# Second pass of the attention scores as 64-row matmuls on the two halves of the array, with every second tile of keys stored with its parts exchanged

## The chip, the cores and the metric

The kernel runs on one core of one Trainium2 chip. The metric is device time in microseconds, from the first to the last instruction of one execution; the number for a kernel is the median of its runs. Lower is better. PE is TensorE's matmul stream, PEld its weight loads, DVE VectorE, ACT ScalarE, POOL GpSimd, SP the engine that issues nearly all DMAs.

## What is computed

One decoder layer over 2048 tokens of width 1024: a conditioned RMS norm, one wide input projection, an mLSTM group of 4 heads, a differential-attention group of 8 heads, an output projection with a gate, and a final RMS norm. The change touches only the attention group, so this is the part to have in mind:

```python
def diff_attention(q, k, v, lam, rel_bias):
    q = q * (A_QKD ** -0.5)                       # A_QKD = 64, A_VHD = 128
    for blk in range(S // Q_BLOCK):               # 16 blocks of 128 queries
        ke = (blk + 1) * Q_BLOCK
        logits = einsum('bqhmd,bkhmd->bmhqk', q[blk], k[:, :ke])   # m: two maps
        logits = where(causal, logits + bias, -inf)
        p = softmax(logits, axis=-1)
        w = p[:, 0] - lam * p[:, 1]
        outs.append(einsum('bhqk,bkhe->bqhe', w, v[:, :ke]))
```

## The kernel before, in words

**Order of work.** Nothing is issued directly. `Program.note` writes every instruction down with what it reads and writes; `Program.order` then makes a list schedule from the planner's own costs (`Program.cost`, line 141): whenever a modelled engine is free, it takes the first noted instruction whose operands are there. The result is a fixed order for each engine, and the chip runs each engine's list in that order. So a cost in `cost` moves instructions, and changes no duration on the chip. All instructions therefore carry one line of the file, L243, and groups are told apart by the names of tiles.

**Stages.** `phase_a(0)` projects queries, keys, values and gates of the first 1024 tokens, `attention(0)` treats query blocks 0 to 7 of all heads, `phase_a(1)` and `attention(1)` do the same for the second 1024 tokens and blocks 8 to 15, and then come the mLSTM stages and the output projection. The scheduler mixes neighbouring stages: while attention waits for other engines, PE takes projection matmuls (PSUM tiles `ps_pj`), which are noted later and so have lower priority.

**Precision.** Every projected value is kept as two parts, hi and lo, both float32r, whose sum is the value. `keep_qk` (line 712) writes the parts of 64 channels of one map to DRAM, `dQ` and `dK`, in the order hi, lo.

**Scores** (`attention`, lines 854 to 875). For a head, K is loaded so that partitions 0 to 63 hold its hi part and 64 to 127 its lo part (`Kt`, in the arena `ar`). Q is loaded twice, so that `Qt[:, m, 0]` holds Q hi in both halves, and `Qt[:, m, 1]` Q lo in both. One tile of up to 512 keys takes two matmuls into one bank of PSUM: the first gives Q hi times (K hi + K lo), the second adds Q lo times (K hi + K lo). The banks `ps_S` are four, taken in turn. After a tile's second matmul DVE takes its minimum (`tensor_reduce` or `tensor_tensor_reduce`, into `mn`); after the last tile of a map ACT takes the exponential of every tile, which frees the banks. A query block has 1 to 4 tiles.

**What follows.** The weights `w` are turned on PE (`ps_tr`), split into parts, and multiplied by V (`ps_pv`).

Of the kernel before, what the change touches and what calls it, by code (L numbers as in the profile page):

```python
# [14 lines left out]
DRAM = bass.MemoryType.DRAM  # L15

P = 128
# [50 lines left out]


class Lane:  # L70
    """One engine's instruction stream: calls are noted down, not issued."""

    def __init__(self, prog, name):
        self.prog, self.name = prog, name
# [5 lines left out]


class Program:
    """Notes the kernel's instructions with what they read and write, then issues them in the
    order of a list schedule: whenever an engine is free it takes the first noted instruction
    whose operands are there."""

    LANES = ("tensor", "vector", "scalar", "gpsimd", "sync")
    COLD = 32000.0
# [52 lines left out]
    def cost(self, lane, method, out, ins, kwargs):  # L141
        n = self.width(out)
        if lane == "sync":
            return 530.0
        if lane == "tensor":
            if method == "transpose":
                return 109.0
            if ins[0].dtype == F32R:
                return max(108.0, 3 + n / 2.4)
            return 2 * max(108.0, 3 + n / 1.2)  # L150
        if lane == "scalar":
            aps = sum(isinstance(kwargs.get(k), bass.AP) for k in ("scale", "bias", "accum_out"))
            return 51.0 + n / 1.2 + 93.0 * aps
        n = max(n, max((self.width(a) for a in ins), default=0))
        if lane == "gpsimd":
            if kwargs.get("op") == ALU.pow:
                return 300.0 + 165.0 * n
            return 150.0 + n * (2.1 if method == "tensor_tensor" else 0.9)
        scalars = [a for a in ins if self.width(a) == 1]
        if method in ("tensor_scalar", "tensor_copy") and "PSUM" not in str(ins[0].space):  # L160
            return 68.0 + n * 0.53
        if method == "reciprocal":
            return 60.0 + n * 8
        return 68.0 + n * 1.042 + (62.0 if scalars else 0.0)
# [81 lines left out]
class K:  # L246
# [172 lines left out]
        nc.vector.tensor_scalar(tmp, src, scale, EPS, op0=ALU.mult, op1=ALU.add)  # L419
        nc.gpsimd.tensor_tensor(dst, tmp, self.half[:, :n], op=ALU.pow)  # L420

# [1 line left out]
    def ht(self, slot, lo):  # L423
        return self.r(self.hs[slot] + lo * 4096, [KT, 512])

# [1 line left out]
        return self.r(W0 + lo * 3136, [KT, 392])  # L427

    def turned(self, n, vecs):
        """vectors over channels, turned so that channels lie on partitions"""  # L430
        nc = self.nc
        parts = vecs[-1][0] + vecs[-1][1].shape[0] // P
        rows = self.f(MST + 512 + n * P, [P], parts=parts)
        if n == 0:
            nc.gpsimd.memset(rows, 0.0)
        for at, src in vecs:
            nc.sync.dma_start(out=rows[at:at + src.shape[0] // P, :], in_=src.rearrange("(k p) -> k p", p=P))
        pt = self.psum("pj" if n == 0 else "tr")
        nc.tensor.transpose(pt[:, 0:parts], rows, self.ident[0:parts, 0:parts])
        nc.vector.tensor_copy(self.cols[:, 72 * n:72 * n + parts], pt[:, 0:parts])  # L440
# [12 lines left out]
        self.gsc = cst.tile([P, KT], F32, name="gsc")  # L453

    def adaln(self, g, on_pe):
        """shift and scale of 256 channels: some of the products on TensorE, the others on VectorE"""
        nc = self.nc
        acc = self.f(SML + 512 * (g % 2), [2, 256])
        m = len(on_pe) + 1
        pm = self.psum("md")[:, 0:4 * m].rearrange("p (q j i) -> p q j i", q=2, j=2)  # L460

        def columns(i, src, vec):
            for q in (1, 0):
                for j in range(2):
                    nc.tensor.matmul(pm[:, q, j, i:i + 1], src[:, q, j * P:(j + 1) * P], vec, start=True, stop=True)

        for k in range(KT):
            slab = self.f((0, 2048, MST)[(2 * g + k // 4) % 3] + k % 4 * 512, [2, 256])
            rows = self.i["w_ada"][0, k * P:(k + 1) * P, 0:2048]
            nc.sync.dma_start(out=slab, in_=rows.rearrange("p (q c) -> p q c", q=2)[:, :, g * 256:(g + 1) * 256])  # L470
            sc = self.sc[:, k:k + 1]
            if k in on_pe:
                columns(on_pe.index(k), slab, sc)
            elif k == 0:
                nc.vector.tensor_scalar(acc, slab, sc, None, op0=ALU.mult)
            else:
                nc.vector.scalar_tensor_tensor(acc, slab, sc, acc, op0=ALU.mult, op1=ALU.add)
        columns(m - 1, acc, self.ones[:, 0:1])
        ks = slice(2 * g, 2 * g + 2)
        for q, dst in ((1, self.gsc), (0, self.shift)):  # L480
            if m > 1:
                nc.vector.tensor_reduce(dst[:, ks], pm[:, q], axis=AX.X, op=ALU.add)
            nc.vector.tensor_tensor(dst[:, ks], dst[:, ks] if m > 1 else pm[:, q, :, 0],
                                    self.cols[:, 32 + 8 * q + 2 * g:34 + 8 * q + 2 * g], op=ALU.add)
        nc.vector.scalar_tensor_tensor(self.gsc[:, ks], self.gsc[:, ks], 1.0,
                                       self.cols[:, 64 + 2 * g:66 + 2 * g], op0=ALU.add, op1=ALU.mult)

    def load_x(self, tg):
        """x of four token tiles, scaled by its reciprocal root mean square"""
        nc = self.nc  # L490
        x = self.i["x"][0]
        junk = self.f(TMP, [1024])
        ss, tmp, rr = (self.hst[:, q, 4 * tg:4 * tg + 4] for q in range(3))
        for j in range(4):
            t = tg * 4 + j
            xt = self.f((0 if tg == 1 else 4096) + 1024 * j, [1024])
            nc.sync.dma_start(out=xt, in_=x[t * P:(t + 1) * P, :])
            nc.scalar.activation(junk, xt, AF.Square, accum_out=ss[:, j:j + 1])
            self.rsqrt(rr[:, j:j + 1], ss[:, j:j + 1], 1.0 / D, 1, tmp[:, j:j + 1])
            nc.vector.tensor_scalar(xt, xt, rr[:, j:j + 1], None, op0=ALU.mult)  # L500
# [29 lines left out]
                                           in_=self.dH[tg][lo][:, q:q + 2, :])  # L530

    def out_gate(self):
        """the output gate on all partitions, kept in DRAM"""
        nc = self.nc
        ga, gb = self.f(4096, [1024]), self.f(5120, [1024])
        for k in range(KT):
# [12 lines left out]
        nc.sync.dma_start(out=self.dB, in_=gb)  # L549

    def gate_weights(self):
        """the gates' columns, beside the last slot of the weight ring"""
        nc = self.nc
        gw = self.f(TMP + 1024, [KT, 8])
        nc.sync.dma_start(out=gw, in_=self.i["w_in"][0, :, C_MI:C_MI + 8].rearrange("(k p) c -> p k c", p=P))
# [84 lines left out]
        nc.scalar.activation(self.g_ws, self.g_ws, AF.Exp)  # L640
        nc.scalar.activation(self.g_dc, self.g_dc, AF.Exp)

# [1 line left out]
    def fill_w(self, c0, hi, lo, eng=None):  # L644
        nc = self.nc
        raw = self.f(RAW + (self.nw % 2) * 1024, [KT, P])
# [12 lines left out]
        return self.wring(0)[:, :, cs], self.wring(1)[:, :, cs]  # L659

    def load_w2(self, c0, *slots):
        """256 columns in one load: two slots of the ring, or one wide one"""
        nc = self.nc
        raw = self.f(RAW, [KT, 256])
        nc.sync.dma_start(out=raw, in_=self.i["w_in"][0, :, c0:c0 + 256].rearrange("(k p) c -> p k c", p=P))
# [6 lines left out]
        return ws  # L672

    def proj_c(self, w, slot, name):
        """channel-major block: [128 channels, 512 tokens]"""
        pj = self.psum("pj", name)
        self.proj_k(pj, w, slot, range(KT))
        return pj
# [8 lines left out]
            nc.tensor.matmul(pj, lo[:, k, :], h0[:, k, :], start=False, stop=(k == KT - 1))  # L687

    def proj_t(self, w, slot, j2, name):
        """token-major block: two tiles of [128 tokens, 256 columns]"""  # L690
        pj = self.psum("pj", name)
        for j in range(2):
            self.proj_r(pj[:, j * 256:(j + 1) * 256], w, slot, 2 * j2 + j)
# [15 lines left out]
            o = MST + self.nst * 1024  # L709
        return self.f(o, [512], F32R), self.f(o + 512, [512], F32R), self.f(o, [2, 512])  # L710

    def keep_qk(self, pj, dst, tg, scale, at=None):
        nc = self.nc
        hi, lo, both = self.stage_a(at)
        self.split(hi, lo, pj, scale)
        ts = slice(tg * 512, (tg + 1) * 512)
        for m in range(2):
            nc.sync.dma_start(out=dst[2 * m:2 * m + 2, :, ts].rearrange("s p c -> p s c"),
                              in_=both[64 * m:64 * m + 64])

    def phase_a(self, half, mid, first=()):
        nc = self.nc
        tgs = (2 * half, 2 * half + 1)
        stage = self.stage_a

        def heads_qk(c0, slots, dsts, scale, ws):
            done = ws is not None
            for w, dst in zip(ws or self.load_w2(c0, *slots), dsts):
                for tg in tgs[1:] if done else tgs:
                    self.keep_qk(self.proj_c(w, tg % 2, ""), dst, tg, scale)  # L730

        def head_z(h, w):
            for tg in tgs:
# [8 lines left out]
        for pr in range(AH // 2):  # L742
            h0 = 2 * pr
            pre = (first[0:2], first[2:4]) if first and pr == 0 else (None, None)
            heads_qk(C_AQ + P * h0, (c, a), self.dQ[h0:h0 + 2], -0.125, pre[0])
            heads_qk(C_AK + P * h0, (1, c), self.dK[h0:h0 + 2], 1.0, pre[1])
            w, = self.load_w2(C_AV + 256 * pr, min(a, 1))
            if pr == 1:
                w = tuple(self.wring(j)[:, :, P:] for j in range(2))
# [24 lines left out]
                break  # L774
        self.wa, self.wc = a, c

# [1 line left out]
    def bias_tiles(self):  # L778
        nc, cst = self.nc, self.cst
        rb = cst.tile([33, AH], F32, name="rb")  # L780
# [9 lines left out]
        for h in range(AH):  # L790
# [3 lines left out]
            nc.vector.tensor_copy(sb, pb[:, 0:384])  # L794
            dst = self.dT[h].rearrange("(p c) -> p c", c=513)[:, 0:384]
            nc.sync.dma_start(out=dst, in_=sb)

    def attention(self, half):
        nc, cst = self.nc, self.cst
# [25 lines left out]
        for h in range(AH):  # L825
# [7 lines left out]
            for pi in range(4 * half, 4 * half + 4):  # L833
# [7 lines left out]
                for bq in range(2):  # L841
# [12 lines left out]
                    for m in range(2):  # L854
# [1 line left out]
                        mn, nm = mnt[sid2], nmt[sid2]  # L856
                        pts = []
                        npart = 0
                        for (a, bnd) in tiles:
                            pt = self.psum("S", f"ps_S{h}_{i}_{m}_{a}")  # L860
                            pts.append(pt)
                            for s in range(2):
                                nc.tensor.matmul(pt[:, 0:bnd - a], Qt[:, m, s, bq * P:(bq + 1) * P],
                                                 Kt[:, m, a:bnd], start=(s == 0), stop=(s == 1))
                            f1 = min(bnd, Fc)
                            if f1 > a:
                                nc.vector.tensor_reduce(mn[:, npart:npart + 1], pt[:, 0:f1 - a], axis=AX.X, op=ALU.min)
# [63 lines left out]
                nc.vector.scalar_tensor_tensor(c_, turned, self.anw, zt, op0=ALU.mult, op1=ALU.mult)  # L931
                nc.sync.dma_start(out=self.dA[pi // 2][:, h, (pi % 2) * 256:(pi % 2 + 1) * 256], in_=c_)

# [1 line left out]
    def stage_m(self):  # L935
        self.nst = (self.nst + 1) % 3
        o = (MST, MST + 1040, TMP)[self.nst]
# [72 lines left out]
        for n in range(8):  # L1010
            self.zo(half, n, *((c, a), (1, c), (a, 1))[n % 3])

# [1 line left out]
    def mlstm_buffers(self):  # L1014
        nc, cst = self.nc, self.cst
        self.ml_f = (self.f(0, [8, P]), self.f(1024, [4, 256]), [self.f(2048 + 512 * j, [4, P]) for j in range(2)],
# [222 lines left out]
```

## Time and profile before

| | |
|---|---|
| median of 3 runs | 2996.12 us |
| lowest and highest | 2994.66 and 2997.53 us |
| the profiled execution: span from first to last instruction | 2997.5 us |
| PE busy | 2849.1 us (95%) in 16032 matmuls |
| PEld busy | 2454.4 us (82%) |
| DVE, ACT, POOL busy | 1649.4, 1351.0, 914.4 us |

The profiled execution is as long as the slowest of the three runs and 1.4 us above their median. "Busy" for PE counts a matmul from its start to a modelled end, and matmuls overlap in it: a record of 0.40 us follows the one before it after 0.23 us. So what one matmul costs in a row of its kind is read from the distance of starts, not from the duration. A weight load (PEld) normally lies under the matmul before it. "issue" as the cause of idle time means that the engine waited for nothing that the profile shows.

### The profile page before, as it was taken

What the parts mean: (1) busy time and instruction counts of PE and PEld (TensorE: products, weight loads), DVE (VectorE), ACT (ScalarE), POOL (GpSimd) and SP (SyncE); (2) the same over time, 40 slices, a digit from 0 to 9 for tenths busy, and PEclk for the clock granted to TensorE, in tenths of its full rate; (3) what the DMA queues carried; (4) which work ended last, traced back from release to release, by engine and by line L of the source; (5) the groups of instructions that cost most, each with busy time, mean ns of one, the idle gap of its engine ahead of it and who ended that gap; (6) DMA issues with size and microseconds to landing.
All of it is one profiled execution on the core that took longest, in us unless ns stands there. A gap on an engine that the chain in (4) does not pass through costs nothing.

```text
span 2997.5 us, 43354 instructions
## 1 busy us (share of the span) xinstructions
PE 2849.1 (95%) x16032; PEld 2454.4 (82%) x16032; DVE 1649.4 (55%) x3378; ACT 1351.0 (45%) x3355; POOL 914.4 (31%) x594
## 2 busy tenths in 40 slices
PE   7999999999999999999999999999989889999999
PEld 5878888888888888798887888788788877878887
DVE  6123327776711557766866767866777575232222
ACT  4111325565611455565655656664554454221211
POOL 3112232322312232231221232233544454243332
PEclk9999999999999999999999999999999999999999
DMA  7356667666654632334253335524433444333332
GB/s 257 110 164 231 222 214 218 176 163 176 182 171 123 210 96 87 100 103 115 75 130 84 109 102 190 148 78 123 133 117 98 143 126 150 103 124 115 126 115 97
DMA packets 407539, 419.96 MB, mean 140 GB/s; under 512 B 19540, under 2 KB 348446, under 8 KB 405278
## 3 DMA queue, kind: packets, MB, share of 16 engines
q1 hardware_dynamic: 407326, 417.19, 46.7%
q8 instruction: 126, 2.06, 0.3%
q14 instruction: 87, 0.71, 0.1%
HBM read 280.77 MB, written 136.35 MB: 139 GB/s over the span
## 4 chain that ended last, share of the span: by engine, by line
PE 75%; DVE 10%; DMA 7%; ACT 3%; issue 3%; POOL 2%; SPq 1%; POOLq 0%; DVEq 0%; ACTq 0%
PE ps_pj L243 51%; PE ps_S L243 12%; DVE af L243 7%; PE ps_pv L243 7%; PE ps_tr L243 5%; DMA ar<-dK 3%; ACT af L243 2%; POOL ar L243 1%; ACT ar L243 1%; DVE ar L243 1%; DMA ar<-dQ 1%; SPq L243 1%; DMA af<-in_w_in_dram 1%; DMA ar<-dV 1%; DVE mn L243 1%
## 5 line engine op out<-in xcount | busy, mean ns | idle before, releaser
L243 PE MATMUL ps_pj<-ar 128*128 128x512 f32 (+2 forms) x9936 | 2162.6, 363 | 6.5 <-POOL ar L243 3.1
L243 PEld LDWEIGHTS ps_pj<-ar 128*128 128x128 f32 x9936 | 1648.1, 190 | 268.7 <-issue 5.3
L243 POOL TENSOR_TENSOR ar<-af,ar 128x1024 fp32r<-128x1024 f32 (+3 forms) x308 | 627.9, 2048 | 1068.6 <-ACT ar L243 934.4
L243 PE MATMUL ps_S<-ar 128*128 128x512 f32 (+4 forms) x2096 | 527.6, 357 | 42.3 <-DMA ar<-dK 22.4
L243 ACT ACTIVATE af<-ps_S,nm 128x512 f32<-128x512 f32 (+2 forms) x608 | 386.8, 642 | 141.4 <-DVE nm L243 92.0
L243 ACT ACTIVATE ar<-af 128x1024 fp32r<-128x1024 f32 (+3 forms) x321 | 285.7, 907 | 342.1 <-PE ps_pj L243 201.7
L243 PEld LDWEIGHTS ps_S<-ar 128*128 128x128 f32 x2096 | 351.2, 197 | 91.4 <-issue 33.7
L243 DVE TENSOR_REDUCE mn<-ps_S 128x1 f32<-128x512 f32 (+3 forms) x512 | 297.6, 589 | 146.5 <-PE ps_S L243 143.6
L243 ACT ACTIVATE af<-ps_pj 128x512 f32<-128x512 f32 (+2 forms) x292 | 171.2, 586 | 431.6 <-PE ps_pj L243 385.4
L243 PE MATMUL ps_pv<-ar 128*128 128x256 f32 (+2 forms) x1920 | 319.7, 283 | 20.4 <-DVE af L243 9.2
L243 POOL TENSOR_SCALAR af<-af,rZ,nlam 128x128 f32<-128x128 f32 (+15 forms) x128 | 168.3, 1315 | 529.4 <-DVE rZ L243 445.8
L243 PEld LDWEIGHTS ps_pv<-ar 128*128 128x128 f32 x1920 | 280.5, 190 | 56.7 <-DVE ar L243 16.2
L243 ACT ACTIVATE ar<-ps_tr 128x512 fp32r<-128x512 f32 (+1 forms) x288 | 165.7, 575 | 236.3 <-PE ps_tr L243 226.0
L243 DVE TENSOR_TENSOR ar<-ps_tr,ar 128x512 fp32r<-128x512 f32 (+1 forms) x288 | 188.8, 656 | 113.4 <-ACT ar L243 112.6
L243 DVE SCALAR_TENSOR_TENSOR af<-af,rZ 128x128 f32<-128x128 f32 (+15 forms) x128 | 193.8, 1514 | 27.6 <-POOL af L243 27.3
L243 DVE SCALAR_TENSOR_TENSOR af<-af,cols 128x512 f32<-128x512 f32 x192 | 189.7, 989 | 30.8 <-ACT af L243 28.8
L243 PE MATMUL ps_tr<-ident,af 128*128 128x128 f32 x1115 | 184.8, 277 | 12.9 <-DVE af L243 12.4
L243 DVE TENSOR_TENSOR af<-ps_pj,af 128x512 fp32r<-128x512 f32 (+3 forms) x103 | 66.3, 643 | 186.1 <-ACT af L243 174.7
L243 ACT ACTIVATE af<-af 128x512 f32<-128x512 f32 (+3 forms) x114 | 78.1, 685 | 181.8 <-DVE af L243 176.7
L243 PEld LDWEIGHTS ps_tr<-ident,af 128*128 128x128 f32 x1115 | 134.4, 142 | 26.3 <-DVE af L243 16.5
L243 POOL TENSOR_TENSOR ss<-ss,half 128x2 f32<-128x2 f32 x64 | 48.9, 764 | 337.4 <-DVE ss L243 286.8
L243 DVE TENSOR_TENSOR ps_pj<-ps_pj,af 128x512 f32<-128x512 f32 (+1 forms) x33 | 22.6, 683 | 206.2 <-PE ps_pj L243 206.2
(135 smaller groups left out, 1748.0 us busy)
## 6 DMA issues: line engine op xcount, KB each, us to landing
af<-in_w_in_dram SPq DMA_DIRECT2D x50, 1024.0 KB, 5.1
ar<-dQ SPq DMA_DIRECT2D x128, 256.0 KB, 4.2
af<-in_w_in_dram SPq DMA_DIRECT2D x44, 512.0 KB, 5.0
af<-in_x_dram SPq DMA_DIRECT2D x32, 512.0 KB, 3.8
dQ<-af SPq DMA_DIRECT2D x64, 256.0 KB, 4.8
dK<-af SPq DMA_DIRECT2D x64, 256.0 KB, 3.9
dV<-af SPq DMA_DIRECT2D x64, 256.0 KB, 2.2
dH<-ar SPq DMA_DIRECT2D x32, 512.0 KB, 6.1
```

The costliest lines, as they stand in the source:

```text
L243: getattr(getattr(nc, lane), method)(*args, **kwargs)
```

## The change

The second matmul of a tile now leaves out Q lo times K lo: it reads only the 64 rows in which K hi lies. For that to be possible on either half of the array, K tiles of every second 512 keys are written to `dK` with their parts exchanged, so that K hi lies in partitions 64 to 127 there. A static method, `aside`, finds neighbouring tiles of which each lies in one block of 512 keys and which lie in opposite kinds of block. Their second matmuls are noted after all first matmuls of the map, as matmuls of 64 rows, one on rows 0 to 63 and one on rows 64 to 127 (the program gives them a tile of 64x128 at row 0 or 64). All other tiles keep the full second matmul, which is right for either order of the parts, since Q lies in both halves. DVE's minima are noted after all of a map's matmuls. The planner is told that a float32r matmul with 64 rows costs 60 + n/4.8 ns, which is 167 ns for 512 columns where the full one is put at 216.

```diff
@@ cost
             if ins[0].dtype == F32R:
+                if ins[0].shape[0] == 64:
+                    return 60 + n / 4.8
                 return max(108.0, 3 + n / 2.4)
@@ keep_qk
-    def keep_qk(self, pj, dst, tg, scale, at=None):
+    def keep_qk(self, pj, dst, tg, scale, at=None, turn=False):
         for m in range(2):
-            nc.sync.dma_start(out=dst[2 * m:2 * m + 2, :, ts].rearrange("s p c -> p s c"),
-                              in_=both[64 * m:64 * m + 64])
+            if turn:
+                for s in range(2):
+                    nc.sync.dma_start(out=dst[2 * m + 1 - s, :, ts], in_=both[64 * m:64 * m + 64, s, :])
+            else:
+                nc.sync.dma_start(out=dst[2 * m:2 * m + 2, :, ts].rearrange("s p c -> p s c"),
+                                  in_=both[64 * m:64 * m + 64])
@@ phase_a (keys only)
-                    self.keep_qk(self.proj_c(w, tg % 2, ""), dst, tg, scale)
+                    self.keep_qk(self.proj_c(w, tg % 2, ""), dst, tg, scale, turn=keys and tg % 2 == 1)
@@ new
+    @staticmethod
+    def aside(tiles):
+        of, ti = [], 0
+        while ti + 1 < len(tiles):
+            (a, b), (c, d) = tiles[ti:ti + 2]
+            if (a // 512 + 1 == c // 512) and (b - 1) // 512 == a // 512 and (d - 1) // 512 == c // 512:
+                of += [ti, ti + 1]
+                ti += 1
+            ti += 1
+        return of
@@ attention
-                        for (a, bnd) in tiles:
+                        qs = slice(bq * P, (bq + 1) * P)
+                        aside = self.aside(tiles)
+                        for ti, (a, bnd) in enumerate(tiles):
                             pt = self.psum("S", f"ps_S{h}_{i}_{m}_{a}")
                             pts.append(pt)
-                            for s in range(2):
-                                nc.tensor.matmul(pt[:, 0:bnd - a], Qt[:, m, s, bq * P:(bq + 1) * P],
-                                                 Kt[:, m, a:bnd], start=(s == 0), stop=(s == 1))
+                            nc.tensor.matmul(pt[:, 0:bnd - a], Qt[:, m, 0, qs], Kt[:, m, a:bnd],
+                                             start=True, stop=False)
+                            if ti not in aside:
+                                nc.tensor.matmul(pt[:, 0:bnd - a], Qt[:, m, 1, qs], Kt[:, m, a:bnd],
+                                                 start=False, stop=True)
+                        for ti in aside:
+                            a, bnd = tiles[ti]
+                            rows = slice(a // 512 % 2 * 64, a // 512 % 2 * 64 + 64)
+                            nc.tensor.matmul(pts[ti][:, 0:bnd - a], Qt[rows, m, 1, qs], Kt[rows, m, a:bnd],
+                                             start=False, stop=True)
+                        for pt, (a, bnd) in zip(pts, tiles):
                             f1 = min(bnd, Fc)
```

What this does to the order of instructions shows at three places. Both programs have 15856 matmuls. The order prints a matmul's output only, so a tile's first matmul and its 64-row second one read alike.

The first place is PE in `attention(1)`: the second map of query block 9 of one head, with tiles of 512, 512 and 256 keys in banks `ps_S2`, `ps_S3` and `ps_S0`. Before:

```order
L243 MATMUL ps_S2_135<-ar_131 128x512 x2
L243 MATMUL ps_pj0_139<-ar_131 128x256
L243 MATMUL ps_pv_138<-ar_131 128x256 x5
L243 MATMUL ps_tr_137<-ident_141,af_132 128x128 x4
L243 MATMUL ps_pj0_139<-ar_131 128x256 x10
L243 MATMUL ps_S3_136<-ar_131 128x512 x2
L243 MATMUL ps_pv_138<-ar_131 128x256
L243 MATMUL ps_pj0_139<-ar_131 128x256
L243 MATMUL ps_pj1_140<-ar_131 128x256 x4
L243 MATMUL ps_S0_133<-ar_131 128x256 x2
```

The same three tiles after the change:

```order
L245 MATMUL ps_S2_135<-ar_131 128x512 x2
L245 MATMUL ps_pj0_139<-ar_131 128x256 x7
L245 MATMUL ps_S3_136<-ar_131 128x512 x2
L245 MATMUL ps_pj0_139<-ar_131 128x256
L245 MATMUL ps_pv_138<-ar_131 128x256
L245 MATMUL ps_pj0_139<-ar_131 128x256 x5
L245 MATMUL ps_S0_133<-ar_131 128x256
L245 MATMUL ps_pv_138<-ar_131 128x256 x5
L245 MATMUL ps_tr_137<-ident_141,af_132 128x128 x4
L245 MATMUL ps_S0_133<-ar_131 128x256
```

The tiles in `ps_S2` and `ps_S3` are a pair of `aside`, but a bank comes free at a time, so the 64-row matmul of each stands right behind its own first matmul, with seven projection matmuls between the two. The second place, also PE in `attention(1)`, is a pair whose two banks (`ps_S3` and `ps_S0`) are free together. Before:

```order
L243 MATMUL ps_S3_136<-ar_131 128x512
L243 MATMUL ps_pv_138<-ar_131 128x256 x5
L243 MATMUL ps_tr_137<-ident_141,af_132 128x128 x4
L243 MATMUL ps_S3_136<-ar_131 128x512
L243 MATMUL ps_S0_133<-ar_131 128x512 x2
```

After:

```order
L245 MATMUL ps_tr_137<-ident_141,af_132 128x128 x4
L245 MATMUL ps_S3_136<-ar_131 128x512
L245 MATMUL ps_S0_133<-ar_131 128x512
L245 MATMUL ps_S3_136<-ar_131 128x512
L245 MATMUL ps_S0_133<-ar_131 128x512
L245 MATMUL ps_pj1_140<-ar_131 128x512 x2
```

Here the two 64-row matmuls stand next to each other. The third place is SP in `phase_a(0)`, the stores of one head's keys (`dK_77`) for two token blocks. Before:

```order
L243 DMA dK_77<-af 64x2x512 x2
L243 DMA af<-in_w_ada_dram 128x1024 x2
L243 DMA dK_77<-af 64x2x512 x2
L243 DMA af<-in_w_in_dram 128x8x256
```

After:

```order
L245 DMA dK_77<-af 64x2x512 x2
L245 DMA af<-in_w_ada_dram 128x1024 x2
L245 DMA dK_77<-af 64x512 x4
L245 DMA af<-in_w_in_dram 128x8x256
```

The second token block is stored part by part, in four DMAs instead of two.

## Rows read from the trace of the kernel before

**Rows 1.** The page: span, and the chain that ended last by engine and line.

```profile
span 2997.5 us, 43354 instructions
...
PE 75%; DVE 10%; DMA 7%; ACT 3%; issue 3%; POOL 2%; SPq 1%; POOLq 0%; DVEq 0%; ACTq 0%
PE ps_pj L243 51%; PE ps_S L243 12%; DVE af L243 7%; PE ps_pv L243 7%; PE ps_tr L243 5%; DMA ar<-dK 3%; ACT af L243 2%; POOL ar L243 1%; ACT ar L243 1%; DVE ar L243 1%; DMA ar<-dQ 1%; SPq L243 1%; DMA af<-in_w_in_dram 1%; DMA ar<-dV 1%; DVE mn L243 1%
```

**Rows 2.** Busy time by stretch, from:to, length, engines (instructions), clock, DMA share.

```profile
450.00:840.00 390.00, 366.32 (x2258) 323.20 (x2257) 270.97 (x843) 231.85 (x736) 114.99 (x111) 0.98 0.68 184
975.00:2030.00 1055.00, 1015.53 (x5926) 882.14 (x5925) 737.13 (x1434) 608.53 (x1644) 275.49 (x143) 0.99 0.40 116
```

**Rows 3.** PE's groups by shape: count, busy us, mean ns, idle before.

```profile
L243 PE MATMUL ps_pj<-ar 128*128 128x512 f32 x6768 | 1734.5, 399 | 6.4 <-POOL ar L243 3.1 <-DVE ar L243 2.0 <-ACT af L243 0.7
```

**Rows 4.** PE's timeline near 1100 us: start, length, group, count.

```profile
1100.29 0.62 PE L243 MATMUL ps_S<-ar 128*128 128x512 f32 x2
1100.75 0.40 PE L243 MATMUL ps_pj<-ar 128*128 128x256 f32 x2
```

**Rows 5.** PE's timeline from 150 us, with matmuls of 73 and 33 rows.

```profile
149.77 4.32 PE L243 MATMUL ps_pj<-ar 128*128 128x512 f32 x18
153.93 0.23 PE L243 MATMUL ps_tr<-ident,af 73*128 73x73 f32 x1
153.96 3.26 PE L243 MATMUL ps_pj<-ar 128*128 128x512 f32 x13
...
160.68 6.74 PE L243 MATMUL ps_pj<-ar 128*128 128x512 f32 x28
167.35 0.91 PE L243 MATMUL ps_tr<-af 33*128 33x384 f32 x2
168.19 5.12 PE L243 MATMUL ps_pj<-ar 128*128 128x512 f32 x21
173.24 0.91 PE L243 MATMUL ps_tr<-af 33*128 33x384 f32 x2
174.08 3.53 PE L243 MATMUL ps_pj<-ar 128*128 128x512 f32 x14
```

**Rows 6.** PE's timeline: single matmuls around 159.5 to 160.7 us, three answers.

```profile
159.51 0.40 PE L243 MATMUL ps_pj<-ar 128*128 128x512 f32 x1
159.84 0.59 PE L243 MATMUL ps_tr<-af 33*128 33x384 f32 x1
...
160.27 0.48 PE L243 MATMUL ps_tr<-af 33*128 33x384 f32 x1
160.68 0.50 PE L243 MATMUL ps_pj<-ar 128*128 128x512 f32 x1
```

**Rows 7.** PEld's timeline near 153.7, 159.8 and 845.4 us; brackets: idle before.

```profile
153.70 0.14 PEld L243 LDWEIGHTS ps_tr<-ident,af 73*128 73x128 f32 x1
...
159.84 0.29 PEld L243 LDWEIGHTS ps_tr<-af 33*128 33x128 f32 x2 [0.36 <-issue]
160.68 0.30 PEld L243 LDWEIGHTS ps_pj<-ar 128*128 128x128 f32 x2 [0.55 <-issue]
...
845.35 0.08 PEld L243 LDWEIGHTS ps_pv<-ident,af 64*1 64x1 f32 x1 [0.36 <-issue]
```

**Rows 8.** Whom PE waited for (us, times, longest): 450 to 840, 975 to 2030.

```profile
PE ps_tr L243 <- DVE af L243: 6.3, 3, 3.8
PE ps_S L243 <- DMA ar<-dQ: 5.8, 5, 2.2
...
PE ps_S L243 <- DMA ar<-dK: 18.9, 6, 3.9
PE ps_tr L243 <- DVE af L243: 6.1, 4, 2.3
PE ps_pv L243 <- DVE ar L243: 5.7, 9, 1.6
```

**Rows 9.** SP's issues of key stores: count, minimum/median/maximum ns, first and last start.

```profile
L243 SPq DMA_DIRECT2D dK<-af x64: 574/599/2579, 67.2 to 958.3; - x64
```

More of the change, by code (lines that the diff above doesn't have):

```diff
@@ L724, in phase_a, with heads_qk @@
         stage = self.stage_a
-        def heads_qk(c0, slots, dsts, scale, ws):
+        def heads_qk(c0, slots, dsts, scale, ws, keys=False):
             done = ws is not None
@@ L745, in phase_a @@
             heads_qk(C_AQ + P * h0, (c, a), self.dQ[h0:h0 + 2], -0.125, pre[0])
-            heads_qk(C_AK + P * h0, (1, c), self.dK[h0:h0 + 2], 1.0, pre[1])
+            heads_qk(C_AK + P * h0, (1, c), self.dK[h0:h0 + 2], 1.0, pre[1], True)
             w, = self.load_w2(C_AV + 256 * pr, min(a, 1))
```

## Prediction

> **What bounds the kernel now.** I read the chain of work that ended last first. PE holds 75% of it, 51% in projection matmuls and 12% in the scores [rows 1]. Then the two stretches in which attention runs: in 450 to 840 us PE is busy 366.3 of 390 us, in 975 to 2030 us 1015.5 of 1055, at a granted clock of 0.98 and 0.99, that is nearly all at the upper of its two levels; no other engine passes 271 and 737 us [rows 2]. So PE idles 23.7 and 39.5 us there, 63 in all, and the rest of the stretches is PE at work. The scheduler fills attention's waits with projections, so PE time that is taken away or added in attention goes nearly one to one into the span. What counts is what a 64-row matmul costs PE, with all that it does to its neighbours.
>
> **What one matmul costs today.** A run of 18 projection matmuls of 512 columns takes 4.32 us [rows 5], and one record is 0.40 long [rows 3], so they start (4.32 - 0.40)/17 = 0.23 us apart. The two matmuls of a score tile take from 1100.29 to 1100.75, again 0.23 each [rows 4]. Weight loads cost nothing in such a run because they lie under the matmul before.
>
> **What is removed.** The cut of each query block into tiles (in the code) gives pairs in blocks 5 to 15: one pair in blocks 5 to 12, two in 13 to 15, so 14 for a head and map, 224 in all: 144 of 512 and 512 keys, 48 of 512 and 384, 32 of 512 and 256. If the two second matmuls of each pair ran at the same time, the shorter of each would vanish: 144 x 0.23 + 48 x 0.17 + 32 x 0.115 = 45 us (0.17 and 0.115 are 0.23 by width). That is the most that this change can give.
>
> **Where the pairs stand.** They mostly don't stand as pairs. The four banks come free one by one, and a list schedule takes what is ready: the second matmul of the first tile is ready before the first matmul of the next one. Counted over PE's whole order after the change, the 448 64-row matmuls fall into 406 groups: 370 of one, 30 of two and 6 of three. So there are only 448 - 406 = 42 places where two of them follow each other; the first of the order excerpts is the common case, the second the rare one. A 64-row matmul alone between full ones streams as many columns as the full one did, so it saves nothing by itself.
>
> **What is added: 406 times into the 64-row form and out again.** The trace has no float32r matmul of 64 rows. Its nearest rows are the eight pairs of 33-row float32 matmuls of the bias tiles, which stand alone among full projection matmuls. One of them [rows 6]: the last full matmul starts at 159.51, and the next starts at 159.84, 0.33 later instead of 0.23: 0.10 lost. The first 33-row record is 0.59 long and the second 0.48, as its weight load, 0.11, is bare. The second starts 0.43 after the first, of which 0.11 is that load, so one streams for 0.32. From the second to the next full matmul it is 160.68 - 160.27 = 0.41, 0.09 more than the stream; and that full matmul's record is 0.50 instead of 0.40, again a bare weight load. 0.10 + 0.11 + 0.09 + 0.10 = 0.40 us. PEld shows the same as idle time with no cause but "issue", 0.36 going in and 0.55 going out [rows 7]. A longer count agrees: from 160.68 to 168.19 us lie 28 full matmuls and two of 33 rows, 7.51 us; 28 x 0.23 is 6.46 (by the unrounded 0.2306) and 2 x 0.32 is 0.64, so 0.41 is left; from 168.19 to 174.08 5.89 - 21 x 0.2306 - 0.64 is 0.41 again [rows 5].
>
> Is that the row count, or the switch from float32r to float32? A 73-row float32 transpose among the same matmuls has its load at 153.70, under the matmul before, and the next projection starts at 153.96, 0.03 after it [rows 5, 7]: the type costs nothing. And two matmuls of 64 rows with a one-column weight show the same 0.36 of idle weight loading before them [rows 7]. So I take 0.41 us for each group. What speaks against it is only that none of these has float32r moving data; the price is bounded by 0 (no switch cost for float32r; a gain in the switch itself has no mechanism) and 0.41, and I take 0.41, since a neighbour in type (73 rows) costs nothing and neighbours in rows (33 and 64) cost alike.
>
> On this the Trainium skill speaks against the change: "TensorEngine Tiling (Array Packing)", Key Properties, says that changing the tiling mode drains TensorE. The rows above agree, with 0.10 and 0.09 us for the two drains and a bare weight load behind each, which the page does not price.
>
> **The sum on PE.** 406 x 0.41 = 166 us. At the 42 neighbours the second matmul has its load behind the first one's, 0.11 later, and if it runs beside it, starts 0.11 instead of 0.23 after it: 42 x 0.12 = 5 us back (0 if they don't overlap, 42 x 0.23 = 10 if wholly). Together +161 us on PE, 156 to 166.
>
> **What of it is covered.** Of the 63 us for which PE idles in attention, 18.9 + 5.8 are waits for K and Q loads [rows 8], which come at the start of a head or block, with no 64-row matmul inside the wait. The other 38 are waits like those for DVE (6.3, 6.1, 5.7 are the largest [rows 8]), whose chains run while PE works at other things; a PE that is later by 0.41 here and there finds more of them done. I let 30 of the 38 go. The ends are 0 and 63. **Moved**: the minima of a map wait a little longer, as they stand behind more of PE's work; DVE has 120 to 318 us to spare in the stretches [rows 2], and PE's projections cover it. The order of the projections changes with the planner's new cost, which I put at +-10 us.
>
> **The extra stores.** 16 key blocks are written with four DMAs instead of two, 32 issues of 0.60 us on SP [rows 9], 19 us in total over some 890 us. Queued behind them are SP's other loads and stores of the projection stage; no wait of PE on the way to the end hangs on them (the dK waits above are for loads at the heads' starts, after all stores of a half). I take 0; the bound is 19 us.
>
> **Sum.** 161 - 30 = +131 on the profiled execution's 2997.5: 3128.5. That execution is 1.4 us above the median of the runs, so 3127 us, slower by 4.4%.
>
> **Rivals.**
> - *No switch price.* The cost belongs to float32 matmuls of few rows [rows 5 to 7], not to the mode. Then only the 42 neighbours matter: 5 to 10 us less, 2986 to 2991. For it: no float32r row of 64 rows exists in the trace. Against: 73 rows. It decides for a gain if the idle before a 64-row weight load stays below 0.01 us in the mean. Chance 0.07, half of it under -0.2%.
> - *All pairs overlap*, 45 us less, 2951. For this PE would have to hold a pair open across the projections that stand between its parts in the order; the order allows that for 42 places. Chance 0.02. Beside this stands the table of theoretical speedup in the Trainium skill, "TensorEngine Tiling (Array Packing)", Overview: up to 2x for up to 64 contracted rows. No run so far shows it.
> - *The waits swallow it.* PE waits for other engines are longer than its idle time shows, since "busy" has modelled ends; the price lands on waits twice as often: +60, 3057. It decides if PE's idle time in attention falls to nearly nothing. Chance 0.07.
> - *Banks are held longer.* A tile's bank is taken from its first matmul on, and the second ends 0.3 us later (0.41 less the way out); where all four banks are in use, the next first matmul waits for the exponential. 11 blocks x 8 heads x 2 maps = 176 maps, each with one such wait of 0.3: +53, 3180. PE's waits for ACT before a score matmul are not among its largest now [rows 8], which speaks against it. Chance 0.10.
>
> **How the numbers follow.** The forecast, 3127, has 0.74. Its own ends are 161 - 63 = +98 and 166 + 0 = +166 with +-10 for the order, so 3085 to 3172. To leave out no more than 0.2, the range goes down to the case in which waits swallow most: 3050 to 3175; out are "no price" and "all overlap" (0.09) and the bank case (0.10). A change of under 0.2% (6 us) can hardly be told from none here: faster by more than that 0.05, within it 0.04, slower 0.91.
>
> **What would show it.** Right: in attention each 64-row weight load has about 0.36 us of idle "issue" before it, and the full one behind it about 0.5; the score groups of 64 rows number 448, PE's idle time plus bare loads grow by some 160 us, all between 450 and 2030 us, and the stretches before and after keep their length. Wrong: 64-row loads that lie under the full matmul before them; starts of 64-row matmuls of one pair within 0.12 us at many places; or a growth outside attention, which would point to the order or to the stores.

## The result, and the profile after

The changed kernel takes 3143.29 us (median of 4 runs, 3135.83 to 3145.74) against 2996.82 us in the same comparison: ratio 1.048, 95% interval 1.0465 to 1.0503. That is 146 us or 4.8% slower. The profiled execution has a span of 3134.1 us, 136.6 more than the one profiled before; the other runs of the changed kernel are 7 to 10 us longer, so the rows below stand for the fast end.

The loss lies in attention. The last store of attention's result (`dA`) is issued by SP at 2068.3 us before and at 2203.7 us after (count, minimum/median/maximum ns, first and last start; the kernel before, then after):

```profile
L243 SPq DMA_DIRECT2D dA<-af x64: 319/332/743, 478.7 to 2068.3; - x64
```

```profile
L245 SPq DMA_DIRECT2D dA<-af x64: 319/332/5741, 480.6 to 2203.7; - x64
```

That is 135.4 of the 136.6 us; what stands behind it kept its length. The page after, which answers [rows 1]:

```profile
span 3134.1 us, 43424 instructions
...
PE 81%; DVE 7%; DMA 5%; issue 3%; POOL 2%; ACT 2%; SPq 0%; POOLq 0%; DVEq 0%; ACTq 0%
```

Busy time in the stretch from 100 us to the end of attention (columns as in [rows 2]):

```profile
100.00:2204.00 2104.00, 2046.63 (x11052) 1628.26 (x11052) 1175.84 (x2513) 974.60 (x2586) 504.58 (x311) 0.99 0.46 136
```

PE's share of the chain grew from 75 to 81%, its idle time there is 2104.0 - 2046.6 = 57 us, less than before, and the granted clock is still 0.99. So PE was given more to do and did not wait more. What it was given shows in PEld's groups by shape (count, busy us, mean ns, idle before and its cause), one group before and two after:

```profile
L243 PEld LDWEIGHTS ps_pj<-ar 128*128 128x128 f32 x9936 | 1648.1, 190 | 268.7 <-issue 5.3 <-POOL ar L243 4.9 <-DVE ar L243 3.0
```

```profile
L245 PEld LDWEIGHTS ps_pj<-ar 128*128 128x128 f32 x9936 | 1629.4, 190 | 315.3 <-issue 70.7 <-POOL ar L245 5.2 <-DVE ar L245 3.0
L245 PEld LDWEIGHTS ps_S<-ar 64*128 64x128 f32 x448 | 75.7, 185 | 114.3 <-issue 111.1
```

The loads of the projections had 5.3 us of "issue" before and have 70.7 after, and the 64-row loads have 111.1. A single group in the timeline of PE, and then in that of PEld (a row of a timeline joins neighbours with the same tiles and prints the shape of the first, so the x2 at 1046.58 is a full matmul and a 64-row one):

```profile
1046.58 0.82 PE L245 MATMUL ps_S<-ar 128*128 128x512 f32 x2
1047.33 0.74 PE L245 MATMUL ps_pj<-ar 128*128 128x512 f32 x2
```

```profile
1046.34 0.19 PEld L245 LDWEIGHTS ps_S<-ar 128*128 128x128 f32 x1
1046.90 0.18 PEld L245 LDWEIGHTS ps_S<-ar 64*128 64x128 f32 x1 [0.37 <-issue]
1047.33 0.53 PEld L245 LDWEIGHTS ps_pj<-ar 128*128 128x128 f32 x3 [0.24 <-issue]
```

The first score matmul starts at 1046.58 with its load just done. The 64-row load starts only at 1046.90, 0.32 later, and the next full load at 1047.33, when the 64-row matmul is through. From the first score matmul to the projection it is 0.75 us instead of the 0.46 of [rows 4], and the projection then still waits for its bare load.

A pair that stands together looks different from what I had expected, on PE and then on PEld:

```profile
1433.42 1.33 PE L245 MATMUL ps_S<-ar 128*128 128x512 f32 x4
```

```profile
1433.39 0.19 PEld L245 LDWEIGHTS ps_S<-ar 128*128 128x128 f32 x1
1433.82 0.19 PEld L245 LDWEIGHTS ps_S<-ar 64*128 64x128 f32 x2 [0.24 <-issue]
1434.26 0.19 PEld L245 LDWEIGHTS ps_S<-ar 128*128 128x128 f32 x1 [0.25 <-ACT ar L245]
```

The x4 on PE are a full matmul, the two of 64 rows, and the next full one. Two 64-row loads take 0.19 us together, as long as one: they start 0.003 us apart, and so do their matmuls. In the trace 36 of the 42 neighbours stand so; in each of the six groups of three one start lies 0.33 us behind the one before it, as it does on the same half in the price experiment below.

### The profile page after: what moved, and what is told of

Its sections match the earlier page's. It is cut to its first block, busy times and chain, and to the rows that moved or that the text cites. A ratio compares the mean times of both kernels' runs of the same rounds, so it can differ in the third digit from the quotient of the medians.

```text
span 3134.1 us, 43424 instructions
## 1 busy us (share of the span) xinstructions
PE 2997.9 (96%) x16032; PEld 2437.8 (78%) x16032; DVE 1675.0 (53%) x3378; ACT 1354.5 (43%) x3355; POOL 907.2 (29%) x594
## 4 chain that ended last, share of the span: by engine, by line
PE 81%; DVE 7%; DMA 5%; issue 3%; POOL 2%; ACT 2%; SPq 0%; POOLq 0%; DVEq 0%; ACTq 0%
PE ps_pj L245 54%; PE ps_S L245 15%; PE ps_pv L245 8%; DVE af L245 5%; PE ps_tr L245 5%; DMA ar<-dK 3%; POOL ar L245 2%; DMA af<-dT 1%; DVE ar L245 1%; ACT ar L245 1%; ACT af L245 1%; POOL sm L245 0%; DMA af<-dZ 0%; DVE mn L245 0%; SPq L245 0%
## 5 line engine op out<-in xcount | busy, mean ns | idle before, releaser
L245 PE MATMUL ps_pj<-ar 128*128 128x512 f32 (+2 forms) x9936 | 2196.4, 366 | 6.2 <-POOL ar L245 3.4
L245 PEld LDWEIGHTS ps_pj<-ar 128*128 128x128 f32 x9936 | 1629.4, 190 | 315.3 <-issue 70.7
L245 PE MATMUL ps_S<-ar 128*128 128x258 f32 (+7 forms) x2096 | 593.6, 377 | 33.7 <-DMA ar<-dK 20.2
L245 PEld LDWEIGHTS ps_S<-ar 128*128 128x128 f32 (+1 forms) x2096 | 351.1, 195 | 190.4 <-issue 140.8
L245 ACT ACTIVATE af<-ps_S,nm 128x512 f32<-128x512 f32 (+2 forms) x608 | 385.1, 640 | 194.5 <-DVE nm L245 111.1
L245 PE MATMUL ps_pv<-ar 128*128 128x256 f32 (+2 forms) x1920 | 328.8, 286 | 22.2 <-DVE ar L245 14.2
```

Source lines behind the costliest of these rows:

```text
L245: getattr(getattr(nc, lane), method)(*args, **kwargs)
```

## The experiments

Theory 1: each group of 64-row matmuls among full ones costs PE about 0.40 us for going in and out, whatever the order. Rival 2: the new order, the planner's price and the stores make the loss. Rival 3: each 64-row matmul is slow, not each group. Where two kernels below are said to have the same order, all five engines' lists are equal row by row.

### The 64-row form in the old order

The kernel before, in its own order; the second matmul of the picked tiles reads rows 0 to 63:

```diff
                             for s in range(2):
-                                nc.tensor.matmul(pt[:, 0:bnd - a], Qt[:, m, s, bq * P:(bq + 1) * P],
-                                                 Kt[:, m, a:bnd], start=(s == 0), stop=(s == 1))
+                                rows = slice(0, 64 if s and (a, bnd) in aside else P)
+                                nc.seen = (Qt[:, m, s, bq * P:(bq + 1) * P], Kt[:, m, a:bnd])
+                                nc.tensor.matmul(pt[:, 0:bnd - a], Qt[rows, m, s, bq * P:(bq + 1) * P],
+                                                 Kt[rows, m, a:bnd], start=(s == 0), stop=(s == 1))
...
```

`nc.seen` tells the schedule that the matmul reads the full operands, so that the order stays as it was.

> The kernel before, with every engine's order exactly as before and the stores as before; only the second matmul of the 448 tiles that the change picks reads rows 0 to 63 (for odd blocks of keys too), so it leaves out Q lo times K lo there. Each stands alone between full matmuls: 448 groups. Theory 1 (going into the 64-row form and out costs PE about 0.40 us for each group, whatever the order): 448 x 0.40 = 179 us on PE, of which some 20 to 35 fall on waits: 3140 to 3160 us. Rival 2 (the new order, the planner's cost and the exchanged stores make the loss): 2990 to 3003 us, as before. Rival 3 (each 64-row matmul is slow, not each group): 3140 to 3160, like theory 1.

Measured: 3153.6 us, ratio 1.053 (1.050 to 1.056), 158 us more than before. No order, price or store changed, so rival 2 cannot be the main cause. PE's stretch up to the end of attention, of the kernel before and of this one:

```profile
100.00:2069.00 1969.00, 1897.82 (x11003) 1643.31 (x11003) 1150.91 (x2508) 969.18 (x2583) 511.58 (x310) 0.99 0.50 145
```

```profile
100.00:2220.00 2120.00, 2068.23 (x10974) 1632.79 (x10973) 1162.72 (x2507) 971.45 (x2581) 503.28 (x310) 0.98 0.46 134
```

PE is busy 170.4 us longer and idles 51.8 instead of 71.2, 19 less. 170.4/448 is 0.38 us a group.

### The new order without the 64-row form

The changed kernel in its own order and with its stores, all second matmuls on 128 rows:

```diff
-                if ins[0].shape[0] == 64:
+                if self.cheap:
                     return 60 + n / 4.8
...
+                            nc.cheap = True
...
-                            nc.tensor.matmul(pts[ti][:, 0:bnd - a], Qt[rows, m, 1, qs], Kt[rows, m, a:bnd],
+                            nc.seen = (Qt[rows, m, 1, qs], Kt[rows, m, a:bnd])
+                            nc.tensor.matmul(pts[ti][:, 0:bnd - a], Qt[:, m, 1, qs], Kt[:, m, a:bnd],
                                              start=False, stop=True)
+                            nc.cheap, nc.seen = False, None
```

`nc.cheap` keeps the planner's low price for these matmuls, and with `nc.seen` the order stays that of the changed kernel.

> The changed kernel, with every engine's order and the exchanged stores exactly as changed, but the 448 second matmuls on all 128 rows (Q lo times K lo is computed again). No 64-row matmul is left. Theory 1: 2990 to 3010 us, the loss is gone. Rival 2: 3125 to 3145 us, the loss stays. Rival 3: as theory 1.

Measured: 3026.8 us, ratio 1.0095 (1.0072 to 1.0117). Both numbers missed: most of the loss is gone, but 31 us of it (against 2995.5 in that comparison) stay with full matmuls. So the 64-row form itself costs 3143 - 3027 = 116 us in this order, and rival 2 has a fifth of the loss. The stretch up to the end of attention, and then PE's longest waits in it (us in total, times, longest):

```profile
100.00:2093.00 1993.00, 1904.57 (x11035) 1648.67 (x11034) 1170.46 (x2513) 969.17 (x2585) 505.40 (x311) 0.99 0.49 143
```

```profile
PE ps_S L247 <- DMA ar<-dK: 34.5, 11, 5.3
PE ps_pv L247 <- DVE ar L247: 19.0, 15, 3.4
```

PE idles 88.4 us here, 17 more than before; waits for K loads and for the split weights of `ps_pv` are the largest (22.4 and 7.6 before in the same stretch). With the 64-row form in the same order the idle time is 57.4, so 31 us of these waits were swallowed by a PE that came later, while its busy time rose by 2046.6 - 1904.6 = 142.

### What makes the 31 us: stores, price, or late noting

Exchanged stores alone, full matmuls, PE's order as before (the diff is that of `keep_qk` and `phase_a` in the change):

> The kernel before with only the exchanged stores of every second block of keys (32 DMA issues more on SP, every other engine's order as before, all matmuls full). Of the 31 us by which the changed order with full matmuls is slower than before: if the stores cause them, 3020 to 3030 us; if the planner's price or the late noting does, 2992 to 3002 us.

Measured: 2994.3 us, ratio 0.998 (0.997 to 1.000). The stores cost nothing.

The new noting with the planner's full price, full matmuls (against the kernel that has the new order without the 64-row form):

```diff
-                if self.cheap:
-                    return 60 + n / 4.8
```

> The changed order's kernel with full matmuls (second matmuls of the picked tiles noted after all first ones, exchanged stores), but the planner is told the price of a full matmul for them (216 instead of 167 ns for 512 columns). If the low price makes the 31 us: 2990 to 3005 us. If the late noting (banks and minima) makes them: 3020 to 3030 us.

Measured: 3029.7 us, ratio 1.010 (1.008 to 1.012). The loss stays without the low price.

The low price alone, in the kernel before (`cheap` is set for the second matmul of a picked tile):

```diff
             if ins[0].dtype == F32R:
+                if self.cheap:
+                    return 60 + n / 4.8
                 return max(108.0, 3 + n / 2.4)
```

> The kernel before with only the planner's low price (167 instead of 216 ns) for the second matmuls of the same 448 tiles, noted where they were, all matmuls full, no exchanged stores. If the low price makes the 31 us: 3015 to 3030 us. If not: 2990 to 3003 us. If any new order is as likely to be worse or better by some 20 us, neither this nor the kernel with the full price will match either number.

Measured: 3008.2 us, ratio 1.004 (1.002 to 1.005), between the two numbers. So the late noting goes with the larger part (some 30 us, with either price), and the price by itself with some 9. The two stand in different places, as the stores of `dA` tell, first for the new order with full matmuls, then for the low price alone:

```profile
L247 SPq DMA_DIRECT2D dA<-af x64: 319/332/6173, 480.0 to 2093.0; - x64
```

```profile
L246 SPq DMA_DIRECT2D dA<-af x64: 319/332/3717, 472.8 to 2067.6; - x64
```

With the new order attention ends 25 us later than before (2068.3), and what follows is as long as it was. With the low price alone attention ends when it did, and the 9 us come behind it, so they are no part of the 31. But see below on other orders: two that also have the late noting show no loss, and by what path the late noting makes PE wait here is not shown.

### The price by itself

The kernel before with extra 64-row matmuls among the output projection's full ones, written to banks that nothing reads:

```diff
+                    if k % 4 == 0 and c < NT - 1:
+                        for q, j in enumerate(((0,), (0, 1), (0, 0), (0, 1) * 4)[c // 4]):
+                            hs = slice(64 * j, 64 * j + 64)
+                            nc.tensor.matmul(self.ring["S"][j + 2 * (q // 2 % 2)], ch[hs, k, :], wo(k, 0)[hs, 0:512], start=True, stop=True)
```

> The kernel before, with extra 64-row float32r matmuls of 512 columns among the output projection's full ones, where PE waits for nobody: into banks that nothing reads, about 30 groups of each kind: one alone; two on opposite halves; two on the same half; eight that change halves each time. Read from PE's rows as the distance between the full matmuls around a group, less their 0.23 each. Theory 1: 0.40 + 0.21 = 0.61 to 0.64 for one; the same for two on opposite halves; 0.83 to 0.87 for two on the same half; 0.40 + 4 x 0.21 = 1.26 for eight. Rival 3: 0.62, 1.24, 1.24 and 5.0. If a weight load must wait for the matmul of its own half, eight take 0.3 to 0.4 more than 1.26.

One execution was taken, of 3100.7 us. PE's timeline around one group of each kind: one alone (with the full matmuls before it), two on opposite halves, two on the same half, eight that change halves; and PEld's loads of the third and the fourth:

```profile
2711.07 0.84 PE L243 MATMUL ps_pj<-ar 128*128 128x512 f32 x3
2711.84 0.50 PE L243 MATMUL ps_S<-ar 64*128 64x512 f32 x1
2712.27 0.72 PE L243 MATMUL ps_pj<-ar 128*128 128x512 f32 x2
...
2747.88 0.50 PE L243 MATMUL ps_S<-ar 64*128 64x512 f32 x2
2748.32 0.73 PE L243 MATMUL ps_pj<-ar 128*128 128x512 f32 x2
...
2855.22 0.73 PE L243 MATMUL ps_S<-ar 64*128 64x512 f32 x2
2855.88 0.73 PE L243 MATMUL ps_pj<-ar 128*128 128x512 f32 x2
...
3002.31 1.20 PE L243 MATMUL ps_S<-ar 64*128 64x512 f32 x8
3003.44 0.74 PE L243 MATMUL ps_pj<-ar 128*128 128x512 f32 x2
```

```profile
2855.22 0.29 PEld L243 LDWEIGHTS ps_S<-ar 64*128 64x128 f32 x2 [0.35 <-issue]
...
3002.31 0.77 PEld L243 LDWEIGHTS ps_S<-ar 64*128 64x128 f32 x8 [0.35 <-issue]
```

From the start of the group to that of the next full matmul: 0.43, 0.44, 0.66 and 1.13 us. To each, 0.09 of draining before the group and 0.10 of the bare load behind it are to be added: 0.62, 0.63, 0.85 and 1.32. So a group of two on opposite halves costs what one costs, a second matmul on the same half 0.23 more, and every further pair in the group 0.23 (1.13 - 0.44 over three). This is theory 1 in all four, with the eight 0.06 over its 1.26, since a pair takes 0.23 and not 0.21; rival 3 would have 1.24 for two and 5.0 for eight. The group of one replaces a full matmul of 0.23, so its net price is 0.39 (0.40 by the unrounded starts of the full matmuls around it), and each pair of 512 columns that stands together gives 0.23 back: by this sum one pair loses 0.16, and two in one group gain about 0.07. The banks here are free and nobody reads them, so neither adding to a bank nor waiting for one is needed for the price.

### Pairs held together

In the changed kernel the first 64-row matmul of a pair is held until both first matmuls are placed, and both have priority:

```diff
+                            firsts.append(len(nc.ops) - 1)
...
-                        for ti in aside:
+                        for at, ti in enumerate(aside):
                             a, bnd = tiles[ti]
+                            nc.ahead = 1000000
+                            if at % 2 == 0:
+                                nc.hold = firsts[aside[at + 1]]
...
```

> The changed kernel, but the first 64-row matmul of a pair is held back until the first matmul of the pair's other tile is noted done, and both have priority, so that all 224 pairs stand next to each other in PE's order (rows 0 to 63, then 64 to 127): 224 groups of two. Theory 1 with overlap as the changed kernel's pairs show it (starts 0.003 us apart, one matmul saved, 0.23 us): 224 x (0.40 - 0.23) = 38 us on PE, less a few for waits, more where a bank is held longer: 3015 to 3045 us, still slower than before. Rival 3 (price for each 64-row matmul): 3120 to 3150 us. A gain over before (under 2990) would say that the price is below 0.23.

Measured: 3010.0 us, ratio 1.005 (1.003 to 1.007), a little under the range: 133 us less than the change as made, and still slower than before. The same order in every engine, with full rows:

> The kernel with the pairs held together, every engine's order exactly as there, but with the 448 second matmuls on all 128 rows: no 64-row matmul is left. The one with 64 rows takes 3010. If a group of two on opposite halves costs 0.41 and saves 0.23, 224 groups cost 40 us on PE, a part of which waits swallow: 2970 to 2990 us, so this order would beat the kernel before. If holding the pairs costs nothing and gains nothing, and the 64-row pairs cost 0.07 each: 2990 to 3000 us.

Measured: 2977.1 us, ratio 0.993 (0.991 to 0.995). The 64-row form costs 33 us in this order. 224 groups at 0.39 make 87 us, and the pairs give back at most the 45 us of the prediction's sum by width, since 80 of them are narrower than 512 and 512; that leaves 42. PE's stretch up to the end of attention, with the 64-row form and with full rows, shows it:

```profile
100.00:2123.00 2023.00, 1960.82 (x11189) 1615.69 (x11188) 1174.50 (x2516) 977.75 (x2598) 512.65 (x313) 0.99 0.49 142
```

```profile
100.00:2088.00 1988.00, 1918.93 (x11187) 1663.09 (x11186) 1175.19 (x2516) 977.99 (x2598) 514.36 (x313) 0.99 0.49 145
```

PE is busy 41.9 us longer and idles 62.2 instead of 69.1, so waits swallow 7 of the 42. Even with every pair side by side the form loses to the full matmuls.

All four of a map in one group, where a block has two pairs (176 groups), and the same order with full rows:

```diff
-                            if at % 2 == 0:
-                                nc.hold = firsts[aside[at + 1]]
+                            nc.hold = firsts[aside[-1]]
```

> The kernel with the pairs held together, but in the blocks with two pairs all four 64-row matmuls of a map are held until the last first matmul, so that they make one group (rows 0, 64, 0, 64): 128 groups of two and 48 of four, 176 instead of 224. By the price of a group (0.41 less 0.23 for each pair) PE has 48 x 0.41 = 20 us less than with 224 groups: 2985 to 3000 us, if the later minima cost nothing; up to 3020 if four banks that finish together stall the exponentials. Under 2977 it would beat the held order with full rows, which the price says it cannot: a group of four gains only 0.46 - 0.41 = 0.05.

> The kernel with groups of four (3032 us), every engine's order exactly as there, but all second matmuls on 128 rows. By the price of groups that order has 128 x (0.41 - 0.23) = 23 us for groups of two and 48 x (0.41 - 0.46) = -2 us for groups of four, 21 us on PE, of which waits swallow a quarter or less: 3010 to 3018 us here. If groups of four cost as much as two groups of two, 224 x 0.18 = 40 on PE: 2992 to 3002 us.

Measured: 3032.0 us (1.012, 1.010 to 1.015), above the range, and 3009.9 us (1.005, 1.003 to 1.007) with full rows, at the edge of it. The order is worse than that of the pairs, but the difference of the two, 22 us, is about what the price of groups gives: 176 groups at 0.39 less 45 for the pairs by width is 24, and 21 by the numbers written down beforehand.

### Is holding the pairs good by itself?

The held order with full rows beats the kernel before by 0.7%, a small gain but clear of the noise, and its work is the same. Two kernels ask why. Priority alone, in the kernel before:

```diff
                             for s in range(2):
+                                nc.ahead = 1000000 if s and (a, bnd) in aside else 0
```

> The kernel before, all matmuls full, stores as before; only the second matmuls of the picked tiles get the highest priority in the schedule, noted where they were. If the 20 us that the held pairs gain with full rows come from second matmuls that no other work is put ahead of: 2970 to 2985 us. If they come from holding the pairs, or from chance in the order: 2990 to 3010 us.

Measured: 2985.6 us, ratio 0.997 (0.995 to 0.998), at the edge of the range. Held pairs with priority, but with the stores and prices as before:

> The kernel before, all matmuls full, stores and planner's prices as before; the second matmuls of a pair are held until both first ones are placed, and have priority. If holding pairs is good by itself: 2970 to 2985 us. If the gain of the held order with full rows was an accident of one schedule (that one had the low price and the exchanged stores, and its order differs in most rows): anywhere from 2975 to 3015 us.

Measured: 2999.6 us, ratio 1.001 (1.000 to 1.003): no gain. So holding the pairs is not what made 2977. Seven orders of the same full matmuls now lie at 2977, 2986, 3000, 3008, 3010, 3027 and 3030 beside the 2993.7 to 2999.4 medians of the kernel before: this list schedule scatters from -0.7 to +1.0% with small edits of its notes. The best of them is faster than both kernels; the stores (2994), the price (3008) and the holding (3000) each by itself don't give its 2977. Where its gain lies can be read from the stores of `dA`:

```profile
L246 SPq DMA_DIRECT2D dA<-af x64: 319/332/2864, 471.1 to 2087.6; - x64
```

Attention ends 19 us later than before, with 11187 matmuls in PE's stretch instead of 11003, and what follows takes 888.0 instead of 929.2 us, 41 less. So the order draws work of later stages into attention, and the gain is the difference of the two. The holding with the old stores and prices does the same and gains nothing (attention ends at 2113.0, 885.2 us follow); what makes the one order better is open.

## Why the prediction was right, and where not

The forecast was 3127 us in a range of 3050 to 3175; 3143 came. By its steps:

- **Where the pairs stand** held: 406 groups for 448 matmuls, and single groups as in the timeline at 1046 us.
- **The price of a group** held: 0.41 was taken from float32 matmuls of 33 rows [rows 5, 6]; the float32r price by itself is 0.62 for a group of one, 0.39 to 0.40 more than the full matmul that it replaces. Over 406 groups the 0.01 to 0.02 are 4 to 8 us. The rival "no switch price" fell with the first experiment.
- **The neighbours** were mis-sized: I gave a pair 0.12 us back, with the second load behind the first one. The loads run side by side, and the whole 0.23 comes back, but only at the 36 places where the starts are 0.003 us apart: 8 instead of 5 us. PE's busy time rose by 142 us at equal order, where the sum had 161. The price and the neighbours explain 7 to 11 of these 19 us; the rest is open.
- **What waits swallow** held in size: 30 us by the forecast, 31 in the new order (88.4 to 57.4 us idle). In the old order, whose waits were counted for it, it was 19.
- **The order** is the term that failed: +-10 us round nothing. The new order alone costs 31 us with full matmuls. It and the PE term miss in opposite directions, -19 and +31, and most of the miss of 16 us is their sum; that they offset each other, so that 3127 came this near to 3143, is luck. On the profiled executions, for which the sum was made, it is 3134.1 against 3128.5. I took a list schedule's new order for neutral, and had no row that says how far it may scatter.
- **The stores** held: nothing.
- **The rivals.** That all pairs overlap needed a different order; with it the pairs do overlap wholly, and the time is 3010, not 2951, because each pair still pays its way in and out. That banks are held longer is not shown as a stall for ACT: PE's waits for it before score matmuls were 4.7 us in all, 3.4 before. That the waits swallow twice as much did not come: PE still idles 57 us in attention.
- **The signs to look for.** Idle "issue" before a 64-row load was there, 111.1 us for 448, but 0.25 each, not 0.36: it is 0.17 to 0.19 where a matmul of 128 or 256 columns stands before, and a second one that shares the way in has none. Behind a group I had named 0.5; it is 0.24 at 1047.33. The 0.55 in [rows 7] stands behind two matmuls that ran one after the other, and behind two such of float32r it is longer too (0.36 in the price experiment). The price did not rest on it.

## What to carry to other kernels

A matmul on half the rows is no cheaper by itself; it pays only beside one on the other half, and only if the group is long enough to carry the switch in and out: here 0.39 us net against 0.23 for each pair of 512 columns (less for narrower ones), so two pairs about break even and one loses. Before splitting work into such pairs, count in the scheduled order how many stand together: a schedule that takes whatever is ready leaves most of them alone. And where an edit goes through a list schedule, measure the new order with the old work in it: it can move the time by 1% with no change in what is computed.

## What the runs showed of the hardware

Two float32r matmuls of 64 rows on opposite halves and different banks start 0.003 us apart, loads included, and eight that change halves run at 0.23 us a pair. On the same half the second starts 0.33 us after the first and adds 0.23 us to the group, though its load comes 0.11 after the first load. The switch costs much the same for float32r on 64 rows (0.39 to 0.40 us) and for float32 on 33 rows (0.40 to 0.41 by [rows 5, 6]). The type alone shows no such price: behind a float32 matmul of 73 rows the next full one starts after 0.03 us [rows 5]. The Trainium skill names about 4 ns between the starts of matmuls on different rows ("TensorE: Matmul & The Clock Gate", The mechanism, and Measured speedup vs the span model); the 0.003 us here agree, and an estimate by that figure gives a pair 0.004 us more than one.
